# Seven small moves around TensorE's waits in a one-layer decoder step: opening, first output pair, last gate pair

## The chip, the cores and the metric

The kernel runs on one core of a Trainium2 chip. The metric is the device time of one execution in microseconds (µs), median of several runs. Engines: TensorE (PE in the profile, with its weight loads as PEld), VectorE (DVE), ScalarE (ACT), GpSimd (POOL) and SyncE (SP), which issues most DMAs.

## What is computed

One layer of a hybrid decoder for 1024 prompt tokens and 8 sample tokens, model width 1024, all in float32:

```python
xn = _rmsnorm(x, pre_g)
u, v, z_a, x_b, z_b, g_a, g_b = split(xn @ w_in)
u, vn = gelu(u), _layernorm(gelu(v), ln_g, ln_b)
y_a = u * _chunk_spatial_mix(vn, w_s, b_s) * silu(z_a)
y_b = pool_branch(x_b) * silu(z_b)
m = sigmoid(g_a) * (y_a @ w_pa) + sigmoid(g_b) * (y_b @ w_pb)
h = x + _rmsnorm(m @ w_out, post_g)
e = p @ w_ple
gate = sigmoid(_rmsnorm(h, ple_in_g) @ w_pg)
y = h + _rmsnorm(gate * e, ple_out_g)
```

Also returned are the last normalised chunk of v and the pooling state.

## The kernel before

Every product is made of split operands: an operand becomes a high part (cast) and a low part (difference), and three products stand for one: high by high, high by low, low by high. So a weight needs a ScalarE cast (names ending in h or hi) and a VectorE subtraction (l or lo) before TensorE can use it. Large products use one level of Strassen (`strassen`, L645): seven products P1 to P7 per pair of 128-row tiles, each of 12 matmuls of 512 columns, with the right operands named A11, S1 and so on and the left ones B11, B21, B22, T1 to T4. P1 takes B11, P6 T2, P2 B21, P7 T3, P4 T4, P5 T1, P3 B22. Results lie in PSUM regions r1 to r5. P1 and P2 share r1, and P5 and P3 share r4: P3 adds to r4 after VectorE has read P5 from it (`evacuate`). P1 is read by ScalarE into u; P6 and P7 are added to u by VectorE; P5, P4 and P3 are each added to u and form an output half. P2, with P1 below it, is the fourth half and is read by ScalarE (`direct`).

PSUM is held in two pools: `region` hands out three buffers of two banks (a bank is 512 float32 columns), `bank` two buffers of one bank. A buffer is handed out again when its last reader is done.

The order of the work is a list scheduler's (`Planner`, L56): what `begin` (L1704) writes stands in written order; from then on steps are placed by costs and due times, each step having a preparation (casts), a run (matmuls) and an evacuation. `LAST` and `FIRST` (L1589, L1591) are the orders of the seven products in the last gate pair and in the first output pair. Steps of neighbouring pairs interleave: P1 of a pair stands ahead of P3 of the pair before it.

The stages that the change touches:

- The opening (`begin`). p (names p, pp, ph, pl) is transposed on TensorE, two tiles of tokens at a time (`p_turn`), w_ple (weraw, wehi, welo) is cut (`cut`), and e = p w_ple is made in tiles e(t, n) of 128 tokens by 512 columns (`embed_terms`). Products of constant data (`busy`, tile warm) fill TensorE while it has nothing to do. x is squared and scaled (squares, ms, rstd), transposed (`x_half`, tile pst), and cast into xB11 and xB21; then the first products of V run (tile acc).
- The output stage (`Out`, m by w_out, names wo, mw, tile acct). In the change's words h is its result. `direct` squares the PSUM values for the norm, and then copies them.
- The gate stage (`Embed`, w_pg, names wg, hw, tile acct): ge is gate by e, u the sums, eback and hback are e and h read back, out is ple_out_g, sps and slow belong to the 8 sample tokens, whose gate is made beside that of the prompt. In the last pair P2 runs in two halves of 256 columns (`run_halves`), each followed by ScalarE's read.

Of the kernel before, what the change touches and what calls it, by code (L numbers as in the profile page):

```python
# [9 lines left out]
F32R = mybir.dt.float32r  # L10
# [5 lines left out]
P = 128  # L16
# [291 lines left out]
def hybrid_step(  # L308
# [257 lines left out]
    class Tokens:  # L566
# [6 lines left out]
        like = staticmethod(lambda t: t)  # L573

    def columns(c):

        class Part(Tokens):
            pieces = staticmethod(lambda ps, wide: [(ps[:, c], c)])
        return Part
# [39 lines left out]
    def classical(weights, operand, user):  # L619

        steps, regions = [], {}
        for j in range(2):
            for m in range(2):
                names = [f"A{m + 1}{k + 1}" for k in range(2)]

                def prepare(names=names):
                    for n in names:
                        if n not in weights.ready:
                            weights.prepare(n)

                def run(names=names, j=j, m=m):
                    ps = regions[m, j] = region("acc")
                    for i, n in enumerate(names):
                        product(Features, ps, weights.ready[n], operand, f"B{i + 1}{j + 1}", i == 0, i == 1,
                                late=m == 0)

                def evacuate(j=j, m=m):
                    user.direct(m, j, Features.view(regions[m, j], j == 1))

                steps.append(Step(prepare, run, evacuate))  # L640
        steps[0].loads = lambda: (weights.fetch(), user.loads())
        steps[-1].after.append(user.finish)
        return steps

    def strassen(weights, operand, user, form=Features, order=None):  # L645
# [6 lines left out]
                ("P3", "S4", "B22", "r4"))  # L652
        place = {p: r for p, _, _, r in plan}

        def evacuate(p):
            ps = form.view(at[place[p]], p not in ("P1", "P2", "P4"))
            if p == "P1":
                both = slot("u", form.sums)
                at["u"], at["u7"] = both[:, 0], both[:, 1]
                if form.tail:  # L660
                    nc.gpsimd.memset(at["u"][:, HALF:], 0.0)
                nc.scalar.activation(out=at["u"][:, :HALF], in_=ps, func=AF.Copy)
                return
# [18 lines left out]
        for p, a, b, r in sorted(plan, key=lambda x: order.index(x[0])) if order else plan:  # L682
# [84 lines left out]
    class Moving:  # L767
# [9 lines left out]

        def cut(self, n, k):
# [4 lines left out]
            split(self.raw[n, kk][:, k % 2], *self.at(n, k))  # L783
            if k % 2:
                del self.raw[n, kk]

# [651 lines left out]
    class Out(User):  # L1438
# [205 lines left out]

    def p_turn(h, q):
        if q == 0:
            pcut[h] = slot("ph", (P, 2, HALF), F32R), slot("pl", (P, 2, HALF), F32R)
        hi, lo = pcut[h]
        ps = bank("pp").rearrange("p (k c) -> p k c", k=2)
        for k in range(2):  # L1650
            for t in range(2):
                nc.tensor.transpose(ps[:, k, t * P : (t + 1) * P], praw[h][:, 2 * q + t, k * P : (k + 1) * P], ident)
        c = slice(2 * q * P, (2 * q + 2) * P)
        split(ps, hi[:, :, c], lo[:, :, c])

# [5 lines left out]
    def embed_terms(t, n, terms):  # L1661

        if t == 3:
            e_ps[t, n] = e_ps.get((t, n)) or bank("e")
        elif t not in e_ps:
            e_ps[t] = region("e")
        out = e_ps[t, n] if t == 3 else e_ps[t][:, n]
        todo = left.setdefault((t, n), 6)
# [10 lines left out]
    def embed_out(t, by=None):  # L1679
        e = slot("e", (P, 2, HALF))  # L1680
        if t == 3:
            for n in range(2):
                nc.vector.tensor_copy(e[:, n], e_ps.pop((t, n)))
        elif by is None:
# [19 lines left out]
    def begin():  # L1704
        psl = slot("psamp", (P, PLE))
        p_load(0, 0)
        for i, v in enumerate((pre_g, pool_scale, ple_in_g)):
            dma(vecs[i * NB : (i + 1) * NB, :], v[0].rearrange("(k p) -> k p", p=P), nc.scalar)
        we.fetch(0)
        p_load(0, 1)  # L1710
        we.fetch(1)
        for t in range(4):
# [13 lines left out]
        def busy(n):  # L1726
            ps = bank("warm")
            for _ in range(n):
                nc.tensor.matmul(ps, junk[:, :P], junk, start=True, stop=True)

        busy(5)
# [20 lines left out]
        vps = bank("vecs")  # L1752
        nc.tensor.transpose(vps[:, : 3 * NB], vecs[: 3 * NB, :], ident[: 3 * NB, : 3 * NB])
        nc.vector.tensor_copy(gvec, vps[:, : 3 * NB])
        embed(2)
# [104 lines left out]
```

## Time and profile before

| | µs |
|---|---|
| median of 3 runs (979.35, 979.36, 980.9) | 979.36 |
| the profiled execution | 979.86 |
| its span, first to last instruction | 978.1 |
| TensorE busy | 967.1 (99%) |
| weight loads | 860.1 (88%) |
| VectorE busy | 796.7 (81%) |
| ScalarE busy | 529.7 (54%) |
| GpSimd busy | 76.5 (8%) |

The span is 1.76 µs shorter than the execution's time. Every engine instruction of the kernel goes through one helper and has its line, L301, so instructions are told apart by tiles: `acct<-woB22h,mw` writes acct and reads woB22h and mw. In a timeline a row gives the start, the time from there to the end of the last instruction of the row, the engine, the operation and its tiles, how many instructions (x), and in brackets how long the engine was idle before it and what ended that.

### The profile page before, as it was taken

The page shows a single profiled execution, that of the slowest core. Times are in us where ns is not written, and L with a number is a line of the kernel's source. Part 1 is how long each engine was busy: PE and PEld are TensorE (multiplying, and loading weights), DVE is VectorE, ACT ScalarE, POOL GpSimd, SP SyncE. Part 2 cuts the span into 40 slices and gives each one's busy share as a digit, 9 for nine tenths or more (in the row PEclk, how much of TensorE's full clock was granted, in tenths as well). Part 3 has the DMA queues.
Part 4 walks back from the last instruction along what each step waited for, and adds up shares of the span by engine and source line. Part 5 has one row for each costly group of instructions (what it writes and reads, how often), then busy time and mean ns, then how long its engine had stood idle before and what let it go on. Part 6 is the DMA issues. An engine that isn't in the chain of part 4 may idle for free. (4 is left out here: it accounts for less than half of the span.)

```text
span 978.1 us, 16049 instructions
## 1 busy us (share of the span) xinstructions
PE 967.1 (99%) x6078; PEld 860.1 (88%) x6078; DVE 796.7 (81%) x1258; ACT 529.7 (54%) x895; POOL 76.5 (8%) x143
## 2 busy tenths in 40 slices
PE   9999999999999999999999999999999999999996
PEld 6898999999999999999999999999999986888775
DVE  5894768777789698989897987697799799679687
ACT  7888998565444333344442343562362364877563
POOL 2400000000000000000000100000000001212212
PEclk9999999999999999999999999999999999999999
DMA  9337354322383353665735076974573483889867
GB/s 340 135 121 179 89 153 152 116 101 80 135 283 129 114 189 97 249 217 205 258 119 194 16 260 218 304 283 150 202 276 109 151 323 92 189 275 364 240 185 232
DMA packets 111914, 183.97 MB, mean 188 GB/s; under 512 B 28951, under 2 KB 68335, under 8 KB 111830
## 3 DMA queue, kind: packets, MB, share of 16 engines
q1 hardware_dynamic: 109742, 175.57, 52.9%
q0 software_dynamic: 2048, 7.37, 4.3%
q8 instruction: 48, 0.79, 0.3%
q14 instruction: 28, 0.23, 0.1%
q10 hardware_dynamic: 48, 0.01, 0.0%
HBM read 124.27 MB, written 53.87 MB: 182 GB/s over the span
## 5 line engine op out<-in xcount | busy, mean ns | idle before, releaser
L301 DVE TENSOR_TENSOR u<-acc,u 128x520 f32<-128x520 f32 (+1 forms) x90 | 62.4, 694 | 31.7 <-PE acc L301 29.1
L301 POOL TENSOR_TENSOR rstd<-ms,mhalf 128x1 f32<-128x1 f32 (+1 forms) x36 | 29.3, 851 | 211.5 <-DVE ms L301 201.6
L301 POOL MEMSET u<- 128x8 f32 x35 | 3.9, 112 | 501.9 <-PE acc L301 235.3
L301 ACT ACTIVATE u<-acc 128x512 f32<-128x512 f32 x39 | 23.3, 596 | 26.4 <-PE acc L301 25.7
L301 ACT ACTIVATE paw<-pas 128x512 fp32r<-128x512 f32 x16 | 10.0, 628 | 31.1 <-DVE pas L301 25.8
L301 ACT ACTIVATE pbw<-pbs 128x512 fp32r<-128x512 f32 x16 | 10.0, 628 | 27.9 <-DVE pbs L301 24.6
L301 DVE TENSOR_TENSOR big<-big 128x1024 f32<-128x1024 f32 (+4 forms) x20 | 23.7, 1214 | 0.0
L301 ACT ACTIVATE big<-mix 128x256 f32<-128x256 f32 x32 | 12.1, 383 | 17.4 <-PE mix L301 16.8
L301 PE MATMUL accm<-qh,wpoolw 128*128 128x260 f32 (+1 forms) x96 | 20.9, 320 | 0.0
L301 ACT ACTIVATE big<-v 128x1024 uint16<-128x1024 uint16 x16 | 18.3, 1175 | 3.4 <-DMA v<-vw 3.4
L301 ACT ACT_TABLE_LOAD x13 | 16.7, 1283 | 5.0 <-PE acc L301 2.6
L301 ACT ACTIVATE zbw<-zbs 128x512 fp32r<-128x512 f32 x16 | 10.0, 627 | 16.4 <-DVE zbs L301 12.2
L301 DVE TENSOR_TENSOR acc<-acc,u 128x512 f32<-128x512 f32 (+1 forms) x16 | 11.1, 696 | 8.9 <-PE acc L301 8.9
L301 ACT ACTIVATE gbw<-gbs 128x512 fp32r<-128x512 f32 x16 | 10.0, 625 | 14.6 <-DVE gbs L301 12.5
L301 ACT ACTIVATE zaw<-zas 128x512 fp32r<-128x512 f32 x16 | 10.1, 628 | 13.6 <-PE acc L301 5.1
L301 PEld LDWEIGHTS accm<-qh,wpoolw 128*128 128x128 f32 x96 | 15.6, 188 | 1.9
L301 ACT ACTIVATE gb<-gb 128x1032 f32<-128x1032 f32 (+1 forms) x8 | 6.8, 854 | 19.0 <-DVE gb L301 19.0
L301 ACT ACTIVATE u<-u 128x1032 f32<-128x1032 f32 (+1 forms) x8 | 6.8, 852 | 18.9 <-DVE u L301 18.8
L301 ACT ACTIVATE hw<-hs 128x512 fp32r<-128x512 f32 x16 | 9.9, 627 | 12.9 <-DVE hs L301 8.9
L301 ACT ACTIVATE uw<-us 128x512 fp32r<-128x512 f32 x16 | 10.0, 627 | 12.6 <-DVE us L301 8.3
L301 DVE TENSOR_TENSOR big<-mix,big 128x256 f32<-128x256 f32 x32 | 12.8, 419 | 4.8 <-ACT big L301 4.4
L301 ACT ACTIVATE za<-za 128x1032 f32<-128x1032 f32 (+1 forms) x8 | 6.8, 854 | 17.4 <-DVE za L301 17.3
(665 smaller groups left out, 3608.8 us busy)
## 6 DMA issues: line engine op xcount, KB each, us to landing
ga<-ga SPq DMA_DIRECT2D x16, 516.0 KB
gb<-gb SPq DMA_DIRECT2D x16, 516.0 KB
ya<-za SPq DMA_DIRECT2D x8, 516.0 KB
yb<-zb SPq DMA_DIRECT2D x8, 516.0 KB
x<-in_x_prompt_dram SPq DMA_DIRECT2D x8, 512.0 KB
vraw<-in_w_in_dram SPq DMA_DIRECT2D x8, 512.0 KB
e<-e SPq DMA_DIRECT2D x8, 512.0 KB
garaw<-in_w_in_dram SPq DMA_DIRECT2D x8, 512.0 KB
```

Source lines behind the costliest of these rows:

```text
L301: getattr(getattr(self.nc, e), method)(*args, **kwargs)
```

## The change

It does this:

1. SP fetches w_ple's second half ahead of p's second part.
2. In the opening, p's first two tiles are transposed and cast by halves, the first half's cast on VectorE; one filler product stands between them instead of two behind. p's second two tiles are turned later, among the products of e(0, 1). High and low parts of w_ple are made apart from each other.
3. e's tile 2 has single banks instead of tile 3, and ScalarE reads it; tile 3 has a region, read by VectorE.
4. x's first block (kp = 0) is transposed into two single banks, and the first product of V writes a bank.
5. In the first output pair P5 stands ahead of P4, and the operands T1 and T4 are made in that order.
6. In the output stage `direct` copies first and squares the copy.
7. In the last gate pair, r1 is two single banks of 256 used columns each. P1 too runs in halves, which the planner places apart from each other.

```diff
-        def evacuate(p):
-            ps = form.view(at[place[p]], p not in ("P1", "P2", "P4"))
+        halved = order is not None and order[-1] == "P2"
+        def evacuate(p):
+            ps = None if halved and p == "P1" else form.view(at[place[p]], p not in ("P1", "P2", "P4"))
...
-                nc.scalar.activation(out=at["u"][:, :HALF], in_=ps, func=AF.Copy)
+                for i, c in enumerate(CUTS if halved else ()):
+                    nc.scalar.activation(out=at["u"][:, c], in_=at["r1"][i][:, :QUART], func=AF.Copy)
+                if not halved:
+                    nc.scalar.activation(out=at["u"][:, :HALF], in_=ps, func=AF.Copy)
...
-            def run_halves(a=a, b=b, r=r):
-                for c in (slice(0, QUART), slice(QUART, HALF)):
-                    product(columns(c), at[r], weights.ready[a], operand, b, False, True, True)
-                    user.direct(0, 0, at[r][:, c], c)
-
-            if order and p == order[-1] == "P2":
-                steps.append(Step(lambda a=a: weights.prepare(a), run_halves, nothing))
-            else:
-                steps.append(Step(lambda a=a: weights.prepare(a), run, lambda p=p: evacuate(p)))
+            def run_halves(p=p, a=a, b=b, r=r):
+                new = r not in at
+                if new:
+                    at[r] = [bank("last") for _ in CUTS]
+                for ps, c in zip(at[r], CUTS):
+                    product(columns(c), ps, weights.ready[a], operand, b, new, True, not new)
+                    if p == "P2":
+                        user.direct(0, 0, ps[:, :QUART], c)
+
+            done = nothing if halved and p == "P2" else lambda p=p: evacuate(p)
+            steps.append(Step(lambda a=a: weights.prepare(a), run_halves if halved and r == "r1" else run, done))
...
-                    ps = regions[m, j] = region("acc")
+                    first = m == j == 0
+                    ps = regions[m, j] = bank("acc").unsqueeze(1) if first else region("acc")
...
-        if kp < NB // 2 - 1:
+        if kp == (NB // 2 - 1 if j else 0):
+            ps = [bank("pst") for _ in range(2)]
+        else:
             ps = region("pst")
             ps = [ps[:, kk] for kk in range(2)]
-        else:
-            ps = [bank("pst") for _ in range(2)]
...
-            parts[t].append(square_sum(ps))
-            nc.scalar.activation(out=h_of[t][:, half(j)], in_=ps, func=AF.Copy)
+            o = h_of[t][:, half(j)]
+            nc.scalar.activation(out=o, in_=ps, func=AF.Copy)
+            parts[t].append(square_sum(o))
...
-    FIRST = ("P1", "P7", "P6", "P2", "P4", "P5", "P3")
+    FIRST = ("P1", "P7", "P6", "P2", "P5", "P4", "P3")
...
-    turn_over(woop, l, [*l[2:], c[0], c[1]], ("B11", "T3", "T2", "B21", "T4", "T1", "B22"))
+    turn_over(woop, l, [*l[2:], c[0], c[1]], ("B11", "T3", "T2", "B21", "T1", "T4", "B22"))
...
-        if t == 3:
+        if t == 2:
             e_ps[t, n] = e_ps.get((t, n)) or bank("e")
...
         we.fetch(0)
+        we.fetch(1)
         p_load(0, 1)
-        we.fetch(1)
...
         busy(5)
-        we.cut(0, 0)
-        p_turn(0, 0)
-        we.cut(0, 1)
-        busy(2)
-        for i in (HH, LH):
-            for t in range(2):
-                embed_terms(t, 0, [(0, i)])
-        p_turn(0, 1)
-        for i in (HH, LH):
-            for t in range(2):
-                embed_terms(t, 0, [(1, i)])
+        we.high(0, 0)
+        p_turn(0, 0, (0,), nc.vector)
+        busy(1)
+        p_turn(0, 0, (1,))
+        we.high(0, 1)
+        for k in range(2):
+            we.low(0, k)
+        for k in range(2):
+            for i in (HH, LH):
+                for t in range(2):
+                    embed_terms(t, 0, [(k, i)])
         for t in range(2):
             embed_terms(t, 0, [(0, HL), (1, HL)])
-        we.cut(1, 0)
-        we.cut(1, 1)
-        for t in range(2):
-            embed_terms(t, 1, [(0, HH), (0, LH), (1, HH), (1, LH), (0, HL), (1, HL)])
+        for k in range(2):
+            we.high(1, k)
+        for k in range(2):
+            we.low(1, k)
...
+        embed_terms(0, 1, [(0, HH), (0, LH), (1, HH), (1, LH)])
+        p_turn(0, 1)
+        embed_terms(0, 1, [(0, HL), (1, HL)])
+        embed_terms(1, 1, [(0, HH), (0, LH), (1, HH), (1, LH), (0, HL), (1, HL)])
...
-        embed_out(3)
         vweights[0].prepare("A11")
+        embed_out(3, nc.vector)
```

How the rows move is shown at three places. First, TensorE at the start of the program: fillers (warm), transposes of p (pp) and the first products of e. Before:

```order
L301 MATMUL pp_133<-ident,p_119 128x128 x4
L301 LDWEIGHTS junk
L301 MATMUL warm_134<-junk 128x512
L301 LDWEIGHTS junk
L301 MATMUL warm_134<-junk 128x512
L301 MATMUL e_135<-wehi_129,ph_131 128x512
L301 MATMUL e_136<-wehi_129,ph_131 128x512
L301 MATMUL e_135<-wehi_129,pl_132 128x512
L301 MATMUL e_136<-wehi_129,pl_132 128x512
L301 MATMUL pp_137<-ident,p_119 128x128 x4
```

Now:

```order
L301 MATMUL pp_135<-ident,p_119 128x128 x2
L301 LDWEIGHTS junk
L301 MATMUL warm_136<-junk 128x512
L301 MATMUL pp_137<-ident,p_119 128x128 x2
L301 MATMUL e_138<-wehi_133,ph_128 128x512
L301 MATMUL e_139<-wehi_133,ph_128 128x512
L301 MATMUL e_138<-wehi_133,pl_129 128x512
L301 MATMUL e_139<-wehi_133,pl_129 128x512
L301 MATMUL e_138<-wehi_133,ph_128 128x512
L301 MATMUL e_139<-wehi_133,ph_128 128x512
```

One filler is gone, and the second four transposes stand further on, among the products of e(0, 1).

Second, VectorE in the gate pair before the last, from its two sums for the sample's gate (slow) to its reading of P5 (the second `ge<-acct,u`). Before:

```order
L301 TENSOR_TENSOR hw_1545<-hs_1546,hw_1545 128x512
L301 TENSOR_TENSOR slow_1519<-slow_1518,slow_1519 8x512
L301 TENSOR_TENSOR hs_1547<-big 128x512
L301 TENSOR_TENSOR ge_1451<-eback_1452,ge_1451 128x512 x2
L301 TENSOR_TENSOR u_1531<-acct_1541,u_1531 128x512
L301 TENSOR_SCALAR ms_1527<-ssq_1502,ssq_1526 128x1
L301 SCALAR_TENSOR_TENSOR ge_1451<-ge_1451,rstd_1528,out_1414 128x1024
L301 TENSOR_TENSOR ge_1492<-acct_1543,u_1531 128x512
L301 TENSOR_TENSOR ge_1515<-eback_1516,ge_1515 8x512 x2
L301 TENSOR_TENSOR ge_1492<-acct_1548,u_1531 128x512
```

Now:

```order
L301 TENSOR_TENSOR hs_1548<-big 128x512
L301 TENSOR_TENSOR ge_1452<-eback_1453,ge_1452 128x512 x2
L301 TENSOR_TENSOR ge_1516<-eback_1517,ge_1516 8x512 x2
L301 TENSOR_TENSOR u_1532<-acct_1542,u_1532 128x512
L301 TENSOR_SCALAR ms_1528<-ssq_1503,ssq_1527 128x1
L301 TENSOR_TENSOR ge_1516<-ge_1516,out_1415 8x512
L301 TENSOR_SCALAR ms_1523<-ssq_1521,ssq_1522 8x1
L301 TENSOR_TENSOR ge_1516<-ge_1516,out_1415 8x512
L301 SCALAR_TENSOR_TENSOR ge_1452<-ge_1452,rstd_1529,out_1415 128x1024
L301 TENSOR_TENSOR ge_1493<-acct_1544,u_1532 128x512
L301 TENSOR_TENSOR hw_1553<-hs_1548,hw_1553 128x512
L301 TENSOR_TENSOR ge_1493<-acct_1549,u_1532 128x512
```

The sum `slow` and `hw_1546` change places just ahead of this piece. The sample's mean (`ms` 8x1), its two products with the gain (`ge<-ge,out` 8x512) and one hw operation, which stood behind the reading of P5, stand ahead of it.

Third, TensorE at the same point: P5 of the pair before the last (wgT1) into its region, then P1 of the last pair (wgB11), then P3 of the pair before it (wgB22), into P5's region. Before:

```order
L301 MATMUL acct_1548<-wgT1h_1441,hw_1538 128x512
L301 MATMUL acct_1557<-wgB11h_1392,hw_1542 128x512
L301 MATMUL acct_1557<-wgB11l_1393,hw_1542 128x512
L301 MATMUL acct_1557<-wgB11h_1392,hw_1542 128x512 x2
L301 MATMUL acct_1557<-wgB11l_1393,hw_1542 128x512
L301 MATMUL acct_1557<-wgB11h_1392,hw_1542 128x512
L301 MATMUL acct_1557<-wgB11h_1394,hw_1542 128x512
L301 MATMUL acct_1557<-wgB11l_1395,hw_1542 128x512
L301 MATMUL acct_1557<-wgB11h_1394,hw_1542 128x512 x2
L301 MATMUL acct_1557<-wgB11l_1395,hw_1542 128x512
L301 MATMUL acct_1557<-wgB11h_1394,hw_1542 128x512
L301 MATMUL acct_1548<-wgB22h_1443,hw_1540 128x512
```

Now:

```order
L301 MATMUL acct_1549<-wgT1h_1442,hw_1539 128x512
L301 MATMUL last_1558<-wgB11h_1393,hw_1543 128x256
L301 MATMUL last_1558<-wgB11l_1394,hw_1543 128x256
L301 MATMUL last_1558<-wgB11h_1393,hw_1543 128x256 x2
L301 MATMUL last_1558<-wgB11l_1394,hw_1543 128x256
L301 MATMUL last_1558<-wgB11h_1393,hw_1543 128x256
L301 MATMUL last_1558<-wgB11h_1395,hw_1543 128x256
L301 MATMUL last_1558<-wgB11l_1396,hw_1543 128x256
L301 MATMUL last_1558<-wgB11h_1395,hw_1543 128x256 x2
L301 MATMUL last_1558<-wgB11l_1396,hw_1543 128x256
L301 MATMUL last_1558<-wgB11h_1395,hw_1543 128x256
L301 MATMUL acct_1549<-wgB22h_1444,hw_1541 128x512
```

The first half of P1 stands ahead of P3; the second, into the other bank, follows P3's twelve matmuls.

## Rows read from the trace of the kernel before

**Rows 1.** The page, parts 1 and 2: busy times, and TensorE's granted clock in 40 slices

```profile
PE 967.1 (99%) x6078; PEld 860.1 (88%) x6078; DVE 796.7 (81%) x1258; ACT 529.7 (54%) x895; POOL 76.5 (8%) x143
PEclk9999999999999999999999999999999999999999
```

**Rows 2.** Waits of TensorE over the span: total µs, times, longest

```profile
PE warm L301 <- DVE junk L301: 1.3, 1, 1.3
PE acct L301 <- DVE ms L301: 0.6, 1, 0.6
PE acct L301 <- ACT ge L301: 0.6, 1, 0.6
PE acc L301 <- DVE xB11l L301: 0.3, 1, 0.3
PE acct L301 <- DVE h L301: 0.2, 1, 0.2
```

**Rows 3.** Timeline of TensorE, first 27 µs: start, duration, operation, [idle before]

```profile
1.26 2.32 PE L301 MATMUL warm<-junk 128*128 128x512 bf16 x5 [1.26 <-DVE junk L301]
...
8.47 1.08 PE L301 MATMUL e<-welo,ph 128*128 128x512 f32 x4
9.39 0.39 PE L301 MATMUL e<-wehi,ph 128*128 128x512 f32 x1
...
18.09 3.65 PE L301 MATMUL pst<-ident,x 128*128 128x128 f32 x32
22.01 1.16 PE L301 MATMUL acc<-xB11h,vw 128*128 128x512 f32 x4 [0.27 <-DVE xB11l L301]
```

**Rows 4.** Timelines of ScalarE, GpSimd and VectorE, first 28 µs

```profile
6.23 0.63 ACT L301 ACTIVATE wehi<-weraw 128x512 fp32r<-128x512 f32 x1 [0.83 <-DMA weraw<-in_w_ple_dram]
...
14.90 1.31 POOL L301 TENSOR_TENSOR rstd<-ms,mhalf 128x1 f32<-128x1 f32 x1 [0.85 <-DVE ms L301]
...
20.46 2.73 DVE L301 SCALAR_TENSOR_TENSOR xB11l<-pst,gvec,xB11h 128x512 fp32r<-128x512 f32 x4 [0.89 <-ACT xB11h L301]
```

**Rows 5.** Timeline of all engines around 816 µs, first output pair

```profile
816.05 0.68 DVE L301 TENSOR_TENSOR h<-acct,u 128x512 f32<-128x512 f32 x1
...
816.79 0.50 PE L301 MATMUL acct<-woB22h,mw 128*128 128x512 f32 x1 [0.21 <-DVE h L301]
```

**Rows 6.** Timeline of all engines, 953 µs to the end, last gate pair

```profile
960.03 0.68 DVE L301 TENSOR_TENSOR u<-acct,u 128x512 f32<-128x512 f32 x1
...
960.86 0.47 PE L301 MATMUL acct<-wgT4h,hw 128*128 128x512 f32 x1 [0.62 <-DVE ms L301]
...
968.99 0.39 PE L301 MATMUL acct<-wgB21h,hw 128*128 128x256 f32 x1 [0.56 <-ACT ge L301]
...
970.86 0.42 DVE L301 TENSOR_TENSOR ge<-eback,ge 128x256 f32<-128x256 f32 x1
```

**Rows 7.** Timeline of VectorE, 932 to 957 µs, gate pair before the last

```profile
943.76 0.21 DVE L301 TENSOR_SCALAR ms<-ssq,ssq 128x1 f32<-128x1 f32 x1 [0.34 <-ACT junk L301]
944.72 1.28 DVE L301 SCALAR_TENSOR_TENSOR ge<-ge,rstd,out 128x1024 f32<-128x1024 f32 x1 [0.75 <-POOL rstd L301]
...
947.72 0.67 DVE L301 TENSOR_TENSOR ge<-acct,u 128x512 f32<-128x512 f32 x1
...
948.92 0.20 DVE L301 TENSOR_SCALAR ms<-ssq,ssq 8x1 f32<-8x1 f32 x1
949.04 1.27 DVE L301 TENSOR_TENSOR ge<-ge,out 8x512 f32<-8x512 f32 x2
```

**Rows 8.** Timeline of TensorE, 945 to 952 µs

```profile
948.82 0.39 PE L301 MATMUL acct<-wgB22h,hw 128*128 128x512 f32 x1
```

**Rows 9.** Timelines of SP, ScalarE and VectorE, 924 to 933 µs

```profile
924.41 0.37 SPq L301 DMA_DIRECT2D out_dram<-ge  x1
...
931.52 0.60 ACT L301 ACTIVATE u<-acct 128x512 f32<-128x512 f32 x1 [3.81 <-DMA out_dram<-ge]
...
932.67 0.69 DVE L301 TENSOR_TENSOR hw<-big,hw 128x512 fp32r<-128x512 f32 x1 [4.71 <-ACT hw L301]
```

More of the change, by code (lines that the diff above doesn't have):

```diff
@@ L573, in hybrid_step @@
         like = staticmethod(lambda t: t)
+    CUTS = (slice(0, QUART), slice(QUART, HALF))
     def columns(c):
         class Part(Tokens):
-            pieces = staticmethod(lambda ps, wide: [(ps[:, c], c)])
+            pieces = staticmethod(lambda ps, wide: [(ps[:, :QUART], c)])
         return Part
@@ L776, in fetch, with high @@
                     dma(r[:, k], self.src[(2 * kk + k) * P : (2 * kk + k + 1) * P, n * HALF : (n + 1) * HALF], by)
-        def cut(self, n, k):
+        def high(self, n, k):
             kk = k // 2
@@ L782, in cut, with low @@
                 self.lo[n, kk] = slot(f"{self.name}lo", (P, 2, HALF), F32R)
-            split(self.raw[n, kk][:, k % 2], *self.at(n, k))
-            if k % 2:
-                del self.raw[n, kk]
+            nc.scalar.activation(out=self.at(n, k)[0], in_=self.raw[n, kk][:, k % 2], func=AF.Copy)
+        def low(self, n, k):
+            hi, lo = self.at(n, k)
+            sub(lo, self.raw[n, k // 2][:, k % 2], f32(hi))
         def drop(self, n):
@@ L1643, in hybrid_step, with p_new, p_turn @@
     pcut = {}
-    def p_turn(h, q):
-        if q == 0:
-            pcut[h] = slot("ph", (P, 2, HALF), F32R), slot("pl", (P, 2, HALF), F32R)
+    def p_new(h):
+        pcut[h] = slot("ph", (P, 2, HALF), F32R), slot("pl", (P, 2, HALF), F32R)
+    def p_turn(h, q, ks=range(2), by=None):
         hi, lo = pcut[h]
         ps = bank("pp").rearrange("p (k c) -> p k c", k=2)
-        for k in range(2):
+        for k in ks:
             for t in range(2):
                 nc.tensor.transpose(ps[:, k, t * P : (t + 1) * P], praw[h][:, 2 * q + t, k * P : (k + 1) * P], ident)
-        c = slice(2 * q * P, (2 * q + 2) * P)
-        split(ps, hi[:, :, c], lo[:, :, c])
+        ks, c = slice(ks[0], ks[-1] + 1), slice(2 * q * P, (2 * q + 2) * P)
+        if by is None:
+            split(ps[:, ks], hi[:, ks, c], lo[:, ks, c])
+        else:
+            by.tensor_copy(out=hi[:, ks, c], in_=ps[:, ks])
+            sub(lo[:, ks, c], ps[:, ks], f32(hi[:, ks, c]))
     e_ps = {}
@@ L1666, in embed_terms @@
             e_ps[t] = region("e")
-        out = e_ps[t, n] if t == 3 else e_ps[t][:, n]
+        out = e_ps[t, n] if t == 2 else e_ps[t][:, n]
         todo = left.setdefault((t, n), 6)
@@ L1680, in embed_out @@
         e = slot("e", (P, 2, HALF))
-        if t == 3:
+        if t == 2:
             for n in range(2):
-                nc.vector.tensor_copy(e[:, n], e_ps.pop((t, n)))
+                nc.scalar.activation(out=e[:, n], in_=e_ps.pop((t, n)), func=AF.Copy)
         elif by is None:
@@ L1726, in busy @@
         def busy(n):
-            ps = bank("warm")
+            ps = region("warm")[:, 0]
             for _ in range(n):
                 nc.tensor.matmul(ps, junk[:, :P], junk, start=True, stop=True)
+        for h in range(2):
+            p_new(h)
         busy(5)
-        we.cut(0, 0)
-        p_turn(0, 0)
-        we.cut(0, 1)
-        busy(2)
-        for i in (HH, LH):
-            for t in range(2):
-                embed_terms(t, 0, [(0, i)])
-        p_turn(0, 1)
-        for i in (HH, LH):
-            for t in range(2):
-                embed_terms(t, 0, [(1, i)])
+        we.high(0, 0)
[9 more added lines that the diff above has]
+                    embed_terms(t, 0, [(k, i)])
         for t in range(2):
             embed_terms(t, 0, [(0, HL), (1, HL)])
-        we.cut(1, 0)
-        we.cut(1, 1)
-        for t in range(2):
-            embed_terms(t, 1, [(0, HH), (0, LH), (1, HH), (1, LH), (0, HL), (1, HL)])
+        for k in range(2):
+            we.high(1, k)
+        for k in range(2):
+            we.low(1, k)
+        vps = bank("vecs")
+        nc.tensor.transpose(vps[:, : 3 * NB], vecs[: 3 * NB, :], ident[: 3 * NB, : 3 * NB])
+        nc.vector.tensor_copy(gvec, vps[:, : 3 * NB])
+        embed_terms(0, 1, [(0, HH), (0, LH), (1, HH), (1, LH)])
+        p_turn(0, 1)
+        embed_terms(0, 1, [(0, HL), (1, HL)])
+        embed_terms(1, 1, [(0, HH), (0, LH), (1, HH), (1, LH), (0, HL), (1, HL)])
         norm_root(0)
@@ L1751, in begin @@
         norm_scale(0)
-        vps = bank("vecs")
-        nc.tensor.transpose(vps[:, : 3 * NB], vecs[: 3 * NB, :], ident[: 3 * NB, : 3 * NB])
-        nc.vector.tensor_copy(gvec, vps[:, : 3 * NB])
         embed(2)
```

## The prediction

> **What bounds the kernel.** I read the page first: TensorE is busy for 967.1 of 978.1 µs, and its clock row is full from end to end [rows 1]. So a change can only take idle time from TensorE, add some, or alter what follows its last product. Second, the waits of TensorE: five, together 3.0 µs, one of them the start of the program [rows 2]. The other four are the places that the change touches: 0.3 µs before the first product of V, 0.2 µs in the first output pair, 0.6 µs on VectorE and 0.6 µs on ScalarE in the last gate pair. The reader is to see that little is to be had: 1.7 µs, and with the part of a slot that such a row leaves out (a product of 512 columns lasts 0.39 µs, while four in a row take 1.08, so one starts 0.23 after the other [rows 3]: 0.16 µs each) some 2.3 µs. Third, I followed the timeline around each place for what is late there, and around the places where work is moved for what could become late. The profiled execution took 979.86 µs, its span 978.1 µs; the median of the three runs is 979.36 µs, 0.50 µs lower. The sum is made against 979.86, and what comes out is set on the median.
>
> **The opening up to x's transposes: 0.** p is turned in halves, one filler product goes, w_ple's second part is fetched ahead of p's second. The products of the embedding are the same in number. What orders them is w_ple's second tile: ScalarE waits 0.83 µs for it and casts it at 6.23 µs [rows 4]. Nothing in its own queue is taken from ahead of it, so it lands as before, and the products that need it start at 6.23 + 0.63 = 6.86 µs; before, TensorE went on with the second transposes of p at about that time, which now come later. No gain, no loss. If the piece landed with no wait, 0.83 µs could go; that is the lower end. The upper end: ScalarE now casts p's second part directly ahead of x's squares, one cast more (0.63 µs [rows 4]) in the chain squares, mean, rstd (1.31 µs on GpSimd for the last tile [rows 4]), scaling, transposes at 18.09 µs [rows 3]. I take 0, from −0.8 to +0.6.
>
> **x's first block in single banks: −0.4.** The 32 transposes start at 18.09 µs and last 3.65, 0.11 each, so the next slot is at about 21.6, but the first V product starts at 22.01 [rows 3], held by VectorE's low parts, which run from 20.46 in steps of 0.68 [rows 4]. With a bank per block and the first product in a bank, it needs the first of these alone (done by 21.14). That is 0.4 µs; as later low parts are still produced one by one beside it, I take that, between 0 and 0.5. The copies that move between ScalarE and VectorE here lie beside products.
>
> **First output pair: −0.3.** P3 adds to the region that P5's evacuation reads. That evacuation starts at 816.05, and TensorE starts at 816.79 after 0.21 µs of idle time [rows 5]. P5 is now ahead of P4, whose 12 products take 12 × 0.23 = 2.8 µs, so its evacuation has ended by then: 0.21 plus up to 0.16 of slot. Between 0 and 0.4.
>
> **Copy, then square: 0.** Two ScalarE instructions of one tile change places; the region comes free one square (about 0.6 µs) sooner, at places where TensorE waits for nothing [rows 2].
>
> **Last gate pair, what goes: −1.6.** P4 waits for a region at 960.86 (0.62 + 0.16 = 0.8 µs), because VectorE evacuates P7 only at 960.03 [rows 6]. With r1 in two banks P4 gets the region of P6, evacuated one step sooner: −0.8. The second half of P2 waits at 968.99 for ScalarE's read of the first half in the same bank (0.56 + 0.16 = 0.7 µs, and a late restart) [rows 6]; in its own bank it doesn't: −0.8. P1 as 24 products of half width costs nothing to speak of: half the columns, half the slot.
>
> **Last gate pair, what comes: +2.2.** Only half of P1 now stands ahead of P3 of the pair before, and P3 adds to the region from which VectorE evacuates P5. Before, P1's 12 products covered 12 × 0.23 = 2.8 µs up to 948.82, from 946.06 on, and P5's evacuation ran from 947.72 to 948.39 [rows 7, 8]: 0.43 µs to spare. The change takes 12 × 0.115 = 1.4 µs of that cover, so TensorE arrives at 947.5. And VectorE comes later: the sample's gate is moved ahead. Between its last sum (slow) and P5's evacuation stand now also one hw operation (0.60), the sample's mean (0.12), its two products with the gain (1.20), and a second hw (0.60): 2.5 µs more, in steps read from the two products (1.27 for both, the second 0.67 long), of which 0.34 + 0.75 = 1.1 µs fill idle time [rows 7]. So P5 is evacuated from about 949.1 to 949.75, and P3 starts 2.2 µs late. VectorE can't be early: it is dense from 932.67 on, where it had waited 4.71 µs for ScalarE, which had waited 3.81 µs for an output write to land at 931.52, issued at 924.41 [rows 9]; the change leaves that write and its place in SP's queue alone. Bounds: 0 if VectorE is 2.2 µs sooner, 2.8 if none of the idle time is filled in time and restarts cost.
>
> **After the last product: +0.1.** TensorE's part of the tail is −1.6 + 2.2 = +0.6. Behind it ScalarE reads the last bank and VectorE goes on at 970.86 [rows 6]. VectorE's own chain gets its P3 0.6 µs later too and then is as dense as before, so the end follows TensorE or falls 0.3 behind: +0.1 (0 to +0.4).
>
> **Sum:** 0 − 0.4 − 0.3 + 0 − 1.6 + 2.2 + 0.1 = 0.0. 979.86 + 0.0 on the profiled execution, **979.4** on the median. 0.2% is 1.96 µs: about what a measurement of this kernel can tell from no change. With the terms' ends against each other: 978.2 to 980.6, the likeliest case's own range.
>
> **Rivals.**
> (1) *P3 doesn't wait.* If the output write lands 2.2 µs sooner against TensorE, VectorE runs ahead and P5 is evacuated in time. For: all of VectorE's lateness there comes from that one transfer [rows 9]. Against: its queue is not changed. VectorE's chain then limits the tail, and of the 1.6 about 1.3 is kept (the 1.1 µs of idle time that the sample's gate fills [rows 7], and some 0.2 by which VectorE waits for ScalarE at the end): −0.4 − 0.3 − 1.3 = −2.0, 977.4.
> (2) *w_ple lands early.* Its requests have p's second part behind them instead of in front; if the late piece comes with the others, −0.8: 978.6, and 976.6 together with (1).
> (3) *Slower: the clock rises later.* In the opening the fillers take 0.46 µs each (five in 2.32) and the later products of the same width 0.27 (four in 1.08) [rows 3]: TensorE started at half its rate, 1.2 instead of 2.4 GHz, after it had stood idle, and rose while it worked. The clock row reads full there, so it doesn't show this. Now one filler of seven is gone and the products wait at 4.9 to 6.9 µs. If the rise slips behind the first 12 products of the embedding, they cost 0.19 more each: +2.3, 981.7. It decides if products stand 0.4 µs apart past 7.5 µs. Against: transposes and four products fill most of that stretch. The Trainium skill (TensorE: Matmul & The Clock Gate, section What's actually happening) states the rule, "the default state is throttled, and activity releases the throttle"; by it a filler less can only hurt. The trace agrees as to the two rates; no row here shows a late rise.
> (4) *The change's banks bring nothing:* the first product and P4 find another region late. Then −1.2 of the gains go: 980.6.
>
> **Chances.** Forecast 0.58; (1) 0.22, since the stall hangs on one transfer; (2) 0.10; (3) 0.06; (4) 0.04. Faster by over 0.2% (below 977.4): two thirds of (1), 0.15, 0.03 of (2) with (1), and 0.04 of the forecast's low end: 0.22. Slower (above 981.3): (3), 0.06, and 0.04 where (4) or the forecast meets its upper ends: 0.10. Within: 0.68. The range reaches to (1) and (4) and leaves out (3) and (1) with (2): 977.2 to 980.9.
>
> **What would show it.** Right: the waits of TensorE no longer hold xB11l, the h of the first output pair, or the ge on ScalarE; instead a wait of about 2 µs at P3 (wgB22) of the gate pair before the last, on VectorE, some 950 µs in. Products of the embedding with w_ple's second tile start near 6.9, x's transposes near 18, V near 21.6. Wrong: no wait at that P3 (then 1), or transposes well after 18.4 (then ScalarE's order costs).

## The result and the profile after

The change makes the kernel slower by 0.27%: the median is 983.13 µs (22 runs, 978.77 to 985.95) against 980.24 for the kernel before on the same chips (22 runs, 978.70 to 982.46; the 979.36 above was the median of three); the ratio is 1.0027, 95% interval 1.0019 to 1.0034. The forecast was no change, 979.4 in a range from 977.2 to 980.9; the measured median lies 2.2 above that range. The profiled execution took 984.8 µs, 1.7 above the median, and its span 983.0 is 4.9 longer than before's, so the rows below account for more than the 2.9 by which the medians differ.

The page of the changed kernel, busy times and TensorE's clock, to be read against [rows 1]:

```profile
PE 968.6 (99%) x6089; PEld 863.0 (88%) x6089; DVE 798.0 (81%) x1259; ACT 529.6 (54%) x897; POOL 75.6 (8%) x143
PEclk9999999999999999999999999999999999999999
```

At this grain nothing differs. The waits of TensorE do (total µs, times, longest), against [rows 2]:

```profile
PE acct L301 <- DVE ge L301: 2.5, 1, 2.5
PE acc L301 <- DVE vw L301: 2.0, 1, 2.0
PE warm L301 <- DVE junk L301: 1.3, 1, 1.3
PE pp L301 <- DMA p<-in_p_prompt_dram: 0.2, 1, 0.2
```

All four waits that the change aimed at are gone, as forecast. The wait of 2.5 µs on VectorE's ge is the one that the forecast puts ahead of P3 (wgB22). The 2.0 µs on vw stand in no part of it. Timeline of TensorE around them (start, duration, operation, idle before):

```profile
17.53 3.65 PE L301 MATMUL pst<-ident,x 128*128 128x128 f32 x32
20.94 1.17 PE L301 MATMUL acc<-xB11h,vw 128*128 128x512 f32 x4
...
23.79 0.39 PE L301 MATMUL acc<-xB21h,vw 128*128 128x512 f32 x1
26.17 1.40 PE L301 MATMUL acc<-xB21h,vw 128*128 128x512 f32 x3 [2.00 <-DVE vw L301]
27.37 1.05 PE L301 MATMUL acc<-xB21l,vw 128*128 128x512 f32 x2
28.22 1.86 PE L301 MATMUL acc<-xB21h,vw 128*128 128x512 f32 x4
...
819.05 0.50 PE L301 MATMUL acct<-woB22h,mw 128*128 128x512 f32 x1
...
951.97 0.79 PE L301 MATMUL acct<-wgB22h,hw 128*128 128x512 f32 x1 [2.45 <-DVE ge L301]
952.56 0.63 PE L301 MATMUL acct<-wgB22l,hw 128*128 128x512 f32 x1
952.99 1.05 PE L301 MATMUL acct<-wgB22h,hw 128*128 128x512 f32 x2
```

Up to 23.79 the opening is better than forecast: V starts at 20.94, where the forecast has it near 21.6 and the kernel before at 22.01 [rows 3]. Then TensorE stands 2.0 µs, and afterwards four products take 1.86 instead of 1.08. The same follows the wait at 951.97: one product after the other 0.43 apart instead of 0.23. The engines' busy time and the granted clock by stretch (the column of 1.00, 0.62 and so on is the clock as a share of 2.4 GHz) show TensorE at its lower level there (1.2 GHz, half of the full clock, for part or nearly all of a stretch):

```profile
24.00:26.00 2.00, 0.18 (x1) 0.00 (x0) 2.00 (x1) 2.00 (x5) 1.57 (x1) 1.00 1.76 453
26.00:28.00 2.00, 1.83 (x5) 1.49 (x6) 2.00 (x5) 2.00 (x5) 0.00 (x0) 0.62 0.75 270
28.00:30.00 2.00, 2.00 (x6) 1.53 (x6) 1.45 (x6) 1.77 (x4) 1.22 (x3) 0.53 0.70 252
30.00:32.00 2.00, 2.00 (x10) 1.61 (x9) 1.91 (x6) 1.36 (x3) 2.00 (x4) 1.00 0.83 336
...
953.00:955.00 2.00, 2.00 (x6) 1.60 (x5) 2.00 (x5) 0.00 (x0) 0.00 (x0) 0.52 0.95 170
```

What TensorE waits for at 26.17 is VectorE's subtraction for the low part of the weight quarter A12 (vw). Timelines of VectorE and GpSimd in the changed kernel; big<-xB11h,xB11l is `x_whole`, in which GpSimd adds the two parts of x's first block back together:

```profile
20.82 4.74 POOL L301 TENSOR_TENSOR big<-xB11h,xB11l 128x1024 f32<-128x1024 f32 x2 [4.05 <-DVE xB11l L301]
23.19 2.37 POOL L301 TENSOR_TENSOR big<-xB11h,xB11l 128x1024 f32<-128x1024 f32 x1
...
19.34 2.85 DVE L301 SCALAR_TENSOR_TENSOR xB11l<-pst,gvec,xB11h 128x512 fp32r<-128x512 f32 x4
22.11 1.40 DVE L301 SCALAR_TENSOR_TENSOR xB21l<-pst,gvec,xB21h 128x512 fp32r<-128x512 f32 x2
23.42 2.69 DVE L301 TENSOR_TENSOR vw<-vraw,vw 128x512 fp32r<-128x512 f32 x1
26.04 1.40 DVE L301 SCALAR_TENSOR_TENSOR xB21l<-pst,gvec,xB21h 128x512 fp32r<-128x512 f32 x2
```

and the same in the kernel before:

```profile
24.39 2.99 POOL L301 TENSOR_TENSOR big<-xB11h,xB11l 128x1024 f32<-128x1024 f32 x1
...
24.42 0.68 DVE L301 TENSOR_TENSOR vw<-vraw,vw 128x512 fp32r<-128x512 f32 x1
25.02 1.40 DVE L301 SCALAR_TENSOR_TENSOR xB21l<-pst,gvec,xB21h 128x512 fp32r<-128x512 f32 x2
26.34 2.19 DVE L301 TENSOR_TENSOR vw<-vraw,vw 128x512 fp32r<-128x512 f32 x2
```

A subtraction of 0.68 µs takes 2.69 and ends at 26.11, some 0.5 after GpSimd's second addition (23.19 + 2.37 = 25.56). Before, it took 0.68, and it was the addition that took 2.99 instead of 2.37. So in one kernel VectorE stands behind GpSimd, in the other GpSimd behind VectorE, and the order in the kernel before hung on a few hundredths of a microsecond: GpSimd's first addition ended there at about 24.4, just when VectorE came. At such a margin the recorded starts don't tell who was first: GpSimd's second addition is recorded at 24.39, 0.03 ahead of VectorE, and yet it is the one that was held (the expectations for two runs below read this row as VectorE ahead). In the changed kernel VectorE's first low part starts 1.12 earlier, but its four take 2.85 instead of 2.73 and GpSimd follows 1.48 instead of 1.55 after the first, so VectorE comes 0.23 late. The low parts of x, which read PSUM and only one tensor of SBUF, run beside the additions at their usual 0.7.

The Trainium skill (SBUF — State Buffer, section Who interferes with whom) states this as a rule: a VectorE instruction with two inputs in SBUF contends with a GpSimd instruction that reads SBUF, and one with at most one SBUF input doesn't, unless it runs in a mode that uses both ports; the shared ports are an exclusive lock, and the order of issue decides who blocks. The rows agree: 2.69 against 0.68 for the one, 1.40 for two of the other.

### The profile page after: what moved, and what is told of

It is laid out like the page before. It is cut to its first block, busy times and chain, and to the rows that moved or that the text cites. A ratio compares the mean times of both kernels' runs of the same rounds, so it can differ in the third digit from the quotient of the medians.

```text
span 983.0 us, 16077 instructions
## 1 busy us (share of the span) xinstructions
PE 968.6 (99%) x6089; PEld 863.0 (88%) x6089; DVE 798.0 (81%) x1259; ACT 529.6 (54%) x897; POOL 75.6 (8%) x143
## 5 line engine op out<-in xcount | busy, mean ns | idle before, releaser
L301 PE MATMUL acc<-xB21h,vw 128*128 128x512 f32 x40 | 14.5, 437 | 2.0 <-DVE vw L301 2.0
```

What stands on the lines that cost most here:

```text
L301: getattr(getattr(self.nc, e), method)(*args, **kwargs)
```

## The experiments

**GpSimd's additions later, the last pair undone, both, and the last pair alone.** The first edit makes GpSimd wait for VectorE:

```diff
-        x_whole(0, 0)
-        x_whole(0, 1)
         steps[0].run()
         steps[1].prepare()
+        nc.gpsimd.tensor_copy(out=sm("seen"), in_=f32(vweights[0].ready["A22"][1][:, 3, P - 1 :]))
+        x_whole(0, 0)
+        x_whole(0, 1)
```

> The changed kernel, with GpSimd's two additions for the first block of x made to wait until VectorE has the last low parts of the first four weight quarters (a one-column copy of A22's low part on GpSimd ahead of them). Theory G: in the opening of the changed kernel VectorE's subtraction for A12's low part was held for 2.0 us by GpSimd's second addition, TensorE waited those 2.0 us and then ran some 1.6 us longer at the lower clock level. Then TensorE's wait for vw is gone, the subtraction takes 0.68 us, the granted clock stays at 1.00 from 20 to 30 us, and the time falls by about 3.6 us from the changed kernel's 983.1, to 979.5 (about 0.7 below before's 980.2). Rival C: the lower level comes from what TensorE did earlier in the opening, not from this wait: then the clock still falls between 25 and 30 us and the time falls by 2.0 at most, to 981.1. Rival M: GpSimd's additions, now 5 us later, hold something else (combinations of x's blocks): a new wait on VectorE or on big in the first 50 us, time unchanged at about 983.

Measured: 984.38 (12 runs; before on that chip 980.61 in 35, ratio 1.0020, 1.0003 to 1.0037). Rival M. The wait for vw is gone, but GpSimd works in order, and the powers for the norms of x's second block now stand behind both additions: from 32.17 instead of 28.78. Timeline of TensorE in this run:

```profile
34.37 0.66 PE L301 MATMUL pxe<-ident,xe 8*128 8x8 f32 x8 [1.28 <-DVE ms L301]
...
36.85 1.33 PE L301 MATMUL pst<-ident,x 128*128 128x128 f32 x5 [0.50 <-DVE x L301]
```

Behind them the granted clock is 0.67 from 36 to 38 µs and 0.50 from 38 to 40. The cure cost as much as the ill, so the time says nothing on G. The rows do say something: with no addition running, the subtraction takes 0.68 (from 24.01), and the clock is at 1.00 from 20 to 36 µs.

The second kernel hands out r1 as one region of two banks again and evacuates P1 in one piece:

```diff
...
-                    at[r] = [bank("last") for _ in CUTS]
-                for ps, c in zip(at[r], CUTS):
-                    product(columns(c), ps, weights.ready[a], operand, b, new, True, not new)
-                    if p == "P2":
-                        user.direct(0, 0, ps[:, :QUART], c)
+                    at[r] = form.new()
+                for c in CUTS if p == "P2" else ():
+                    product(columns(c), at[r], weights.ready[a], operand, b, new, True, not new)
+                    user.direct(0, 0, at[r][:, c], c)
+                if p == "P1":
+                    product(form, at[r], weights.ready[a], operand, b, new, True, not new)
```

> The changed kernel with the last pair's P1 and P2 again in one region of two banks, as before the change. Theory T: the change of the last pair costs 3.1 us net (2.45 of wait ahead of P3 of the pair before it, about 1.3 of lower clock behind it and more, less the two waits that it removes). Then the wait for VectorE ahead of wgB22 is gone, the waits of T4 and of P2's second half are back, and the time falls by about 3.1 from 983.1 to 980.0. Rival: the last pair costs only the forecast 0.6 (2.2 less 1.6), and the rest of the end's loss comes with the late start from the opening: then 982.5.

Measured: 982.21 (12 runs), 1.6 over before (ratio 1.0014, 0.9998 to 1.0030), so 1.3 less than the changed kernel's excess of 2.9. The wait ahead of wgB22 is gone, and T4's and P2's waits (0.6 each) are back. The size lies nearer to the forecast's 0.6 than to the 3.1 of theory T. The wait for vw is still there (1.91), as this kernel keeps the opening.

> Both edits at once: GpSimd's additions later, and the last pair as before the change. If theories G and T both hold and add, 983.1 less 3.6 less 3.1, 976.4, about 3.8 below before: faster than both kernels. If the rivals hold (C and the small cost of the last pair), 980.5. If the parts don't add, because the end's waits depend on when the opening ends, something between 977.5 and 980.

Measured: 983.22 (12 runs, 2.6 over before, ratio 1.0018, 1.0003 to 1.0032): above all that was expected of it, since the first edit's new wait (1.28 at pxe) is in it. Against that edit alone (984.38) the old last pair takes 1.2 off.

> The kernel before with the last pair's edit alone (P1 and P2 in two single banks), the opening untouched. Theory T: the wait of about 2.45 us ahead of wgB22 of the pair before the last stands here too, followed by the lower clock level, and the time is 3.1 us over before: 983.3. Rival: the wait needs the opening's delay, or is smaller without it: 980.2 to 981 (the forecast's 0.6 at most).

This one is the kernel before with the change's `run_halves` and its banks alone. Measured: 981.45 (12 runs), 0.84 over before, ratio 1.0007 (0.9991 to 1.0023). The wait at wgB22 stands there too, but at 1.42 µs, and the clock stays up behind it. That leaves no room for the 3.1 of theory T; the forecast 0.6 fits, and so does nothing at all. Why the wait is shorter here than the 2.45 of the changed kernel isn't shown.

**One row of GpSimd moved.** The second try leaves the first addition and puts the second behind the five powers; no other row of any engine changes:

```diff
         x_whole(0, 0)
-        x_whole(0, 1)
         steps[0].run()
...
         for t in range(5, NB):
             norm_scale(t)
+        x_whole(0, 1)
```

> The changed kernel with one row of GpSimd moved: its second addition for x's first block (x_whole(0, 1)) is written behind the five powers for the norms of x's second block. Nothing else changes on any engine, and no instruction is added. Theory G: VectorE's subtraction for A12's low part meets no addition of GpSimd, since the first one ended before it; TensorE's wait for vw (2.0 us) and the lower clock level behind it (1.6 us) go, and unlike the first try the powers are not late, so no new wait stands at pxe or x. TensorE then stands about 1.1 us ahead of before after the opening, and the median falls from 983.1 (2.7 over before) by 3.0 to 3.6, to 0.5 below to 0.3 over before; the runs no longer spread up to 986. Rival C (the clock falls anyway between 25 and 30 us): 2.0 at most. Rival M (another wait in the first 50 us): no gain.

Measured: 980.16 (12 runs) against 980.93 of before (35 runs), ratio 0.9986 (0.9967 to 1.0005): from 2.9 over before to 0.8 below, 3.7 µs for one row, a little more than the 3.0 to 3.6 expected. Timelines of VectorE and GpSimd, and of TensorE behind:

```profile
21.17 2.42 POOL L301 TENSOR_TENSOR big<-xB11h,xB11l 128x1024 f32<-128x1024 f32 x1 [4.09 <-DVE xB11l L301]
...
23.64 0.68 DVE L301 TENSOR_TENSOR vw<-vraw,vw 128x512 fp32r<-128x512 f32 x1
...
23.92 1.42 PE L301 MATMUL acc<-xB21h,vw 128*128 128x512 f32 x4
25.18 0.63 PE L301 MATMUL acc<-xB21l,vw 128*128 128x512 f32 x2
25.64 1.09 PE L301 MATMUL acc<-xB21h,vw 128*128 128x512 f32 x4
...
949.50 0.50 PE L301 MATMUL acct<-wgB22h,hw 128*128 128x512 f32 x1 [2.13 <-DVE ge L301]
...
950.07 0.62 PE L301 MATMUL acct<-wgB22h,hw 128*128 128x512 f32 x2
```

Theory G holds: no addition is running, 0.68 it is, and no wait or lower clock follows. The wait ahead of wgB22 is still there, this time with the clock up behind it. The spread up to 986 became one up to 982.8. That the kernel is faster than before is not shown: the interval holds 1, and this profile's span, 979.2, is 1.1 longer than before's. TensorE stands 0.25 ahead of before at the end of wgT1 of the pair before the last (945.58 against 945.83) and 0.38 behind at its last product (970.42 against 970.04).

> The same, with the last pair's P1 and P2 again in one region as before the change. The last pair alone cost 0.9 in the medians of both ways to isolate it (983.1 to 982.2, and 980.6 to 981.5). Theory: the opening's gain of 1.1, the first output pair's 0.3, no loss at the end: 1.2 to 1.6 below before. If the last pair's cost is noise, the same as the kernel with the one edit.

Measured: 979.33 (12 runs), 1.6 below before, ratio 0.9983 (0.9966 to 1.0001), and 0.83 below the kernel with the one edit. With 0.84, 1.3 and 1.2 above, that is the fourth comparison for the price of the last pair; none is clear of the noise by itself, and all four point the same way.

> The kernel before with the same row of GpSimd moved and nothing else. In its profile VectorE's subtraction began at 24.42 us and GpSimd's second addition at 24.39 could not go ahead until 25.0: the one that came first went ahead, by some 0.03 us. Theory G: in some of before's executions the order of the two is the other way, and those are the ones at 982.3 to 986 (2 of 22 and 11 of 35 runs). Then with the edit no run lies above about 982, the median falls by 0.3 to 1.0, and the lowest stays at 978.5 or so. Rival: the high runs of before have another cause (a DMA that lands late): the spread stays.

Measured: 979.77 (12 runs), 1.2 below before, ratio 0.9988 (0.9971 to 1.0005); eleven of the twelve lie at 979.0 to 981.8, and one at 982.93, which the theory had not expected. It fits G (before's runs above 982.3 were 1 of 22, 11 of 35 and 7 of 35, and 1 of 18 further on), but those have no trace, so that they lost this race is argued, not shown, and 1 run of 12 against such shares settles little.

**P1's halves kept together.** On top of the moved row, the planner takes both halves of P1 as one step:

```diff
...
-        plan.apart()
+        if joined:
+            plan.open = (ps.tensor.name, plan.open[1])
+        else:
+            plan.apart()
...
-                    product(columns(c), ps, weights.ready[a], operand, b, new, True, not new)
+                    product(columns(c), ps, weights.ready[a], operand, b, new, True, not new,
+                            joined=p == "P1" and c is not CUTS[0])
```

> The first of these four, with the last pair's two halves of P1 (still in two single banks) planned as one step, so that both stand ahead of P3 of the pair before and cover VectorE's evacuation of P5. Theory T: the wait of 2.45 us ahead of wgB22 falls to that part which 1.4 us of the second half leave, some 1.0, or nothing, while the waits that the change removed (T4, the second half of P2) stay removed: 0.9 to 2.0 below the first of the four. Rival: the wait moves to the next product (T2 waits for ScalarE's or VectorE's later evacuations) and the time is the same as the first's.

Measured: 979.31 (12 runs, 978.21 to 980.42, the narrowest of the kernels with 12), 1.6 below before, ratio 0.9984 (0.9968 to 0.9999), 0.85 below the first of the four. It beats the changed kernel clearly and the kernel before by a little, with an interval that just leaves out 1. Timelines of TensorE and VectorE near the end:

```profile
948.65 0.50 PE L301 MATMUL acct<-wgB22h,hw 128*128 128x512 f32 x1 [0.25 <-DVE ge L301]
...
968.12 0.28 PE L301 MATMUL last<-wgB21h,hw 128*128 128x256 f32 x1
...
968.18 1.41 DVE L301 SCALAR_TENSOR_TENSOR ge<-ge,rstd,hback 128x512 f32<-128x512 f32 x2
969.50 0.42 DVE L301 TENSOR_TENSOR ge<-eback,ge 128x256 f32<-128x256 f32 x1
...
972.49 1.42 DVE L301 SCALAR_TENSOR_TENSOR ge<-ge,rstd,hback 128x512 f32<-128x512 f32 x2 [0.46 <-issue]
```

and the same in the kernel before:

```profile
970.04 0.28 PE L301 MATMUL acct<-wgB21h,hw 128*128 128x256 f32 x1
...
973.49 1.41 DVE L301 SCALAR_TENSOR_TENSOR ge<-ge,rstd,hback 128x512 f32<-128x512 f32 x2
```

The wait ahead of wgB22 is down to 0.25, and the last product starts 1.92 before that of the kernel before (970.04). But the end comes only 1.00 sooner, 972.49 against 973.49: from the last product to VectorE's last pair it takes 4.37 instead of 3.45. VectorE is busy with the other tile's end when the last quarter comes (0.56 of the 0.92), and 0.46 in front of its last pair is idle time for which the profile shows no releaser. In the changed kernel itself the stretch is 4.28, from 974.25 to 978.53. TensorE stood 0.60 ahead before the last pair (945.23 against 945.83, last product of wgT1), so the banks bring it 1.32, and 0.92 of that is given back by VectorE; this kernel's median equals that with the old last pair (979.33).

**The race lost in the kernel before, and shorter additions.** First the kernel before with a little work on VectorE ahead of the subtraction:

```diff
+        for _ in range(2):
+            nc.vector.tensor_copy(sm("idle"), gvec[:, :1])
         vweights[0].prepare("A12")
```

> The kernel before with two one-column copies (some 0.1 us each) on VectorE ahead of its subtraction for A12's low part; nothing else is changed. In before's profile that subtraction came ahead of GpSimd's second addition by some 0.03 us. Theory G (whichever comes first goes ahead, and a two-operand VectorE instruction on SBUF waits for GpSimd's whole addition): the subtraction now comes second, is held some 2 us to the addition's end, TensorE waits 1.7 to 2.2 us for vw at xB21's products, and then runs at the lower level for some time: the median rises by 2 to 3.7 us over before's, of which part is lost anyway in those of before's executions that lose on their own: plus 1.5 to 3. Rival: the hold has to do with the changed kernel's other edits, and two small copies cost their own 0.2 us: no change.

Measured: 984.09 (7 runs, 983.33 to 985.42) against 979.90 (18 runs), ratio 1.0039 (1.0024 to 1.0054). VectorE and TensorE in this run:

```profile
24.84 0.20 DVE L301 COPY idle<-gvec 128x1 f32<-128x1 f32 x2
24.96 2.77 DVE L301 TENSOR_TENSOR vw<-vraw,vw 128x512 fp32r<-128x512 f32 x1
...
27.79 0.96 PE L301 MATMUL acc<-xB21h,vw 128*128 128x512 f32 x3 [2.10 <-DVE vw L301]
```

Two copies that put the subtraction off by 0.12 µs cost 4.2, more than expected, and every run lies above 983: the loss doesn't need the change's other edits. In this profile, which is of the quickest of the seven runs (983.33), the clock stays up behind the wait. Its 2.1 µs of wait are therefore about half of the 4.2. Its span is 3.4 longer than before's: 0.4 of that stood there ahead of the race, where p landed late (pp at 7.49 instead of 7.06), and 1.1 come behind VectorE's last pair, which starts 2.2 late (975.72 against 973.49). The rest of the 4.2 is not accounted for.

The last kernel is the changed one with each addition in two:

```diff
-        nc.gpsimd.tensor_tensor(out=quarter(kp, j)[:, :, :HALF], in0=hi, in1=lo, op=ALU.add)
+        for k in range(2):
+            nc.gpsimd.tensor_tensor(out=quarter(kp, j)[:, k, :HALF], in0=hi[:, k], in1=lo[:, k], op=ALU.add)
```

> The changed kernel with each of GpSimd's additions for x in two instructions of 512 columns (about 1.2 us each by half of 2.4) and nothing else. Theory G1 (a hold lasts one instruction of GpSimd): VectorE's subtraction for A12's low part waits 1.2 us at most and gets in between two halves; TensorE's wait for vw falls from 2.0 to 1.2 or less, the clock stays up, and the median falls by 2 or more from the changed kernel's 2.8 over before. Theory G2 (VectorE gets in only when GpSimd has nothing queued): the wait stays at about 2.0 and the time at 2.8 over before.

Measured: 981.02 (12 runs, 977.45 to 983.47), 1.1 over before, ratio 1.0008 (0.9993 to 1.0023). VectorE and TensorE:

```profile
24.02 0.99 DVE L301 TENSOR_TENSOR vw<-vraw,vw 128x512 fp32r<-128x512 f32 x1
...
25.06 0.97 PE L301 MATMUL acc<-xB21h,vw 128*128 128x512 f32 x3 [0.30 <-DVE vw L301]
...
949.79 0.50 PE L301 MATMUL acct<-wgB22h,hw 128*128 128x512 f32 x1 [2.12 <-DVE ge L301]
```

and GpSimd, the last of its four additions:

```profile
24.42 1.75 POOL L301 TENSOR_TENSOR big<-xB11h,xB11l 128x512 f32<-128x512 f32 x1
```

G1: the hold ends with GpSimd's current instruction, 0.31 here, though the next one stands right behind it; now that one is held, and takes 1.75 where the first takes 1.28. In the opening the clock stays up, as expected; behind the wait at wgB22 it falls (last section). The fall of 1.8 in the medians is a little short of the 2 expected, and the interval (0.9993 to 1.0023) is too wide to rest on: it is the rows that decide for G1.

## Why the prediction was wrong

Its steps, with what the rows show (profile after against before). A lag is the start of the same product after less that before; the lower clock's 1.6 is 4.22 from 26.17 to the next products on xB11 less the 2.63 that the run with the race lost takes for the same, and its 1.4 is worked out in the last section:

| step | forecast | measured |
|---|---|---|
| opening up to x's transposes | 0 | −0.56 (17.53 against 18.09) |
| x's first block in single banks | −0.4 | −0.51 (3.41 from there to V, against 3.92) |
| VectorE's subtraction behind GpSimd (low parts and products behind that block) | not in the sum | +2.0 of wait and some 1.6 of lower clock |
| first output pair | −0.3 | −0.28 (TensorE's lag at wo's rows 2.54, at woB22 2.26) |
| last pair, what goes | −1.6 | −1.8 (T4 −0.94, P2's second half −0.83) |
| last pair, what comes | +2.2 | +2.45 of wait, and 1.4 of lower clock |
| after the last product | +0.1 | +0.83 (4.28 against 3.45) |

The rows add up to 5.1, and VectorE's last pair starts 5.04 later (978.53 against 973.49).

**The step that failed is the one on x's first block.** Up to x's transposes the opening kept within its bounds (−0.56), and the first product of V gained what the single banks were to bring (−0.51). But that term, "between 0 and 0.5", took it that nothing behind that product would be late: "The copies that move between ScalarE and VectorE here lie beside products." VectorE's moved work was weighed against TensorE alone. The prediction never asked what GpSimd was doing at that time, though the trace of before showed one GpSimd addition of 2.99 beside one of 2.37, and two VectorE subtractions in 2.19 that take 1.28 in the changed kernel. What the runs showed in its place is a hold: 2.0 µs of wait, and some 1.6 of lower clock behind it in that execution. One GpSimd row moved out of the way takes 3.7 off the changed kernel; 0.12 µs put in the way of VectorE costs the kernel before 4.2. As far as the medians can tell, that is the whole of the slowdown: with the row moved in both, the change stands at 980.16 against 979.77, +0.4, which 12 runs of each cannot tell from the forecast 0.0.

**The last pair was right in place, mechanism and nearly in size at TensorE.** The forecast +0.6 for what comes less what goes stands against +0.63 in the trace of the kernel with one row moved, where the clock stays up (0.25 ahead before the pair, 0.38 behind at its last product); the four comparisons of medians, 0.83, 0.84, 1.2 and 1.3, have the end behind it in them. The wait ahead of P3 measured 2.45, 2.13, 2.12, 1.72 and 1.42 in five kernels against the 2.2 worked out, and keeping P1's halves together takes it to 0.25, so half of P1 as cover is what was missing. Two parts were mis-sized: the end behind the last product (+0.1, measured +0.8 to +0.9), where VectorE's own chain was taken to follow TensorE, and the lower clock behind a wait of 2 µs, which no term had.

**The rivals.** (1) didn't come: P3 waits. (2) came in part, in some runs: in the profile after, w_ple's second tile was in time, and the runs above with the same opening waited 0 to 1.2 for it. (3), the late rise of the clock at the start, didn't come: from 7.45 µs four products take 1.10, where four took 1.08 before; the clock did cost time, but after a wait, where the prediction hadn't looked. (4) didn't come: the first product of V and T4 both gained at least what was forecast (−0.51 for −0.4, −0.94 for −0.8). Copy then square wasn't tried alone; with the opening and the first output pair it is worth 0.44 together (979.33 against 979.77, both with the row moved), where 0.7 was forecast; the runs can't tell this from nothing.

## What to carry to other kernels

Before a change moves work on VectorE, list what GpSimd runs at that moment: a VectorE instruction with two SBUF inputs and a GpSimd addition that become ready within some 0.2 µs of each other are a race, and the profile of the kernel before shows only which side won it there. A wait of 2 µs on TensorE, where it bounds the kernel, should be priced once without and once with a lower clock behind it. And a cover is lost when half of a product moves: keep in one step what hides another engine's work.

## What the runs showed of the hardware

The clock behind a wait of TensorE differs between executions. After 2.00 and 2.45 (the changed kernel), 1.91 (old last pair) and 2.12 (additions in halves) it went to the lower level; after 2.10 (race lost), 2.13 (one row moved), 1.72 (additions later) and 1.42 (last pair alone) it stayed at 1.00. The same stretch with additions in halves, then with one row moved (columns as above):

```profile
952.00:954.00 2.00, 2.00 (x6) 1.55 (x5) 1.47 (x3) 0.44 (x1) 0.00 (x0) 0.50 1.04 277
...
952.00:954.00 2.00, 2.00 (x16) 1.89 (x15) 2.00 (x4) 0.73 (x3) 0.00 (x0) 1.00 0.98 287
```

With the lower clock, P3's start to T2's takes 5.65 (changed kernel) and 5.85 (additions in halves), without it 4.28 (one row moved) and 4.33 (last pair alone), so 1.4 to 1.6 µs lie between two executions of like waits. A kernel with two such waits could differ by some 3 µs from one execution to the next; that the spread of the runs comes from this is not shown, as one execution of each kernel has a trace. What decides it isn't shown here either.

The other unexpected thing is that VectorE's scaling of a tile of x, one tensor of SBUF and a scalar per partition, is held by GpSimd too. Timeline of VectorE in the kernel with one row moved, where the addition ran from 31.15 to 33.69 (a tile ahead of it, and the one beside it):

```profile
27.94 0.76 DVE L301 TENSOR_SCALAR x<-x,rstd 128x1024 f32<-128x1024 f32 x1
...
31.51 2.73 DVE L301 TENSOR_SCALAR x<-x,rstd 128x1024 f32<-128x1024 f32 x1
```

0.76 became 2.73, beside work that TensorE doesn't wait for in that profile (0.2 µs in two others), so the moved row is cheap by where it lands, not free. The same section of the Trainium skill's page on SBUF counts such scalings among those that can contend, in a mode that uses both ports; which mode it ran in, no run here shows.
